# Ordering a two-layer hybrid decoder step on the compiler's detailed timing model instead of its simple one

## Chip, cores and metric

The kernel runs on one NeuronCore of a Trainium2 chip, as one program in one launch. The metric is the device time of an execution in microseconds (us); lower is better. The five engines have a stream of instructions each, and work through it in the order in which the compiler put it: TensorE (PE, with PEld for its weight loads), VectorE (DVE), ScalarE (ACT), GpSimd (POOL) and SyncE (SP, which issues most of the DMAs).

## What is computed

One inference step of two decoder layers for a prompt of 1024 tokens and 8 samples of one token each (1032 columns in all), width 1024, everything in float32.

```python
# layer 0
h = rmsnorm(x) @ w_in0                 # 4 HGRN2 heads of 128, 8 forgetting-attention (FoX) heads of 64
o = concat(hgrn2(h), fox(h)) @ w_out0  # hgrn2: chunked recurrence; samples: one step on a cached 128x128 state
x = x + o                              # fox: causal attention with a decay; samples: 512 cached positions each
x = x + convffn(rmsnorm(x))            # 2816 channels, gated, causal depthwise convolution of width 3
# layer 1
u = glu(rmsnorm(x) @ w_pw1)
u = swish(layernorm(dwconv31(u)))      # causal depthwise convolution of width 31
x = x + u @ w_pw2
x = x + convffn(rmsnorm(x))
y = rmsnorm(x)
```

The outputs are y for prompt and samples, and the new caches and states.

## The kernel before

**Matrix products.** Activations lie with channels on partitions and tokens along the row. Each float32 operand is split into a rounded high part and the rest: `split` (L104 to L106) makes the high part `wh` with an ACT copy (L105) and the low part `wl` with a subtraction on DVE or POOL (L106). A product is then three matmuls, high by high, high by low and low by high. Weights come in tiles `wr` of 1024x128 (SP DMA, L110, two buffers); the output weights of the ConvFFNs are `wor`, split into `oh` and `ol`. In the input projection of layer 0 the matmuls are those of L143, tiles `mm` of 512 or 260 columns with three PSUM buffers; from then on they are those of `dense2` (L1034 for the first 512 columns, L1037 for the other 520 in two pieces of 260) and of the ConvFFN's second product (L1175, L1184).

**Work under the dense tiles.** All else is "side work", written as Python generators. Between dense tiles the program takes steps from them at a rate set by hand:

```python
def step(self, n=1.0):                       # L191, class Side
    self.due = min(self.due + n, 2 * n)
    while self.due > 0 and self.q:
        self.due -= self.one()
```

In layer 0's mixer (0 to about 660 us) side work is the attention of four pairs of heads (scores L478 to L483, softmax on DVE L484, transposes L504, weighting L518 to L521), then the recurrence of four HGRN2 heads. Each of these heads has a dense part, whose three results `hf`, `hv` and `hq` are copied out by ACT (L589) into tiles that exist once (pool `hgd`, one buffer), so that the next head's copies wait for the last reader of this head's. The recurrence takes a decay chain on DVE (L645 to L694, with `kl` written at L685), transposes of `kl` (L704), products `pa` (L709, L711), a mask on POOL (L716), outputs `hpo` (L735, L737), and at its end the step for the samples, twice four samples: `vb` (DVE, L748), the product `sp3` (PE, L752), the new states `st` (DVE, L758, four instructions) and the products with `hq` (PE, L763, four columns of `sp2`), after which ACT copies `sp2` out (L766). The samples' attention runs beside it: gathers on POOL (L563), a product and a reduction on DVE over the cached keys (L781, L783), and the values (L883).

Later stages are the gates and the output projection (to about 760 us), the ConvFFN of layer 0 (`mlp`, L1116 to L1227) for either half of the tokens, the GLU and the convolution (taps on POOL L1277/L1278 and on DVE L1287/L1289), and the ConvFFN of layer 1. Means over the channels are matmuls: `mean` (L1042 to L1048) sends each piece of 260 columns through one PSUM buffer, and ACT copies it back to `ha` (L1048) before the next piece may be written:

```python
ps = one("dacc", "mean")                     # L1046
PE.matmul(ps[:, :z - o], mean_d, acc[:, o:z], start=True, stop=True)
ACT.copy(acc[:, o:z], ps[:, :z - o])         # L1048
```

**What sets the order.** The Python code says in which order instructions are issued, and the tile framework doesn't keep to it. When the `TileContext` is left (L1460), it puts the instructions of each engine in order, on a model of how long each takes and when its inputs and buffers are free, and then sets the semaphores. So the order on an engine follows from that model, and the hand-written rates are only its input.

## Time and profile before

| | us |
|---|---|
| median of 3 runs (lowest, highest) | 2617.6 (2612.87, 2620.34) |
| profiled execution, from first to last instruction | 2622.4 |
| PE busy in it | 2518.7 (96%) |
| PEld busy | 2223.7 (85%) |
| DVE busy | 1798.5 (69%) |
| ACT busy | 1232.2 (47%) |
| POOL busy | 746.8 (28%) |

The span of the profiled execution is the only time of its own that is known; it lies 4.8 us above the median. An engine is busy while one of its instructions runs; the rest of its span it waits for another engine, for a DMA or for its turn. Where PE is busy at half the clock, its work takes twice as long, so that busy time and useful time differ. The column PEclk of the profile shows that.

### The profile page before, as it was taken

The numbers are of one execution on the slowest core, as the hardware profiler recorded it, in microseconds if no ns is written. First come the engines' busy times: TensorE is split into PE (matmuls) and PEld (weight loads), VectorE is DVE, ScalarE is ACT, GpSimd is POOL, SyncE is SP. The second block draws the span as 40 slices with busy tenths as digits, with TensorE's granted clock in tenths as the row PEclk, the third lists the DMA queues.
The fourth block names the chain that finished last, engine by engine and source line by source line (L and its number), as shares of the span: only waits on it lengthen the run. The fifth ranks groups of instructions, "written<-read, shape, count | busy, mean of one in ns | idle before, by whom it ended". The sixth has DMA issues, their size and how long they took to land.

```text
span 2622.4 us, 40803 instructions
## 1 busy us (share of the span) xinstructions
PE 2518.7 (96%) x15857; PEld 2223.7 (85%) x15857; DVE 1798.5 (69%) x3138; ACT 1232.2 (47%) x2119; POOL 746.8 (28%) x714
## 2 busy tenths in 40 slices
PE   7999998998999999999999999999999999999998
PEld 7788887876787888797799999997777798999997
DVE  7676668776565555577999566759999656655455
ACT  5455565654454333345454345545554643333332
POOL 2011225325131111115664131046664101111111
PEclk9999999999999999999999999999999999999999
DMA  6212225334433333323232322333233323333321
GB/s 200 68 57 57 66 74 151 96 94 144 139 105 98 97 96 96 96 66 104 81 92 87 92 83 72 95 93 101 77 89 97 96 82 102 113 93 90 89 83 59
DMA packets 319908, 247.07 MB, mean 94 GB/s; under 512 B 12055, under 2 KB 292039, under 8 KB 319683
## 3 DMA queue, kind: packets, MB, share of 16 engines
q1 hardware_dynamic: 308899, 213.09, 27.7%
q0 software_dynamic: 10816, 31.38, 4.0%
q8 instruction: 125, 2.05, 0.3%
q14 instruction: 68, 0.56, 0.1%
HBM read 226.82 MB, written 18.73 MB: 94 GB/s over the span
## 4 chain that ended last, share of the span: by engine, by line
PE 70%; DVE 13%; DMA 6%; issue 5%; POOL 3%; ACT 3%; SPq 0%; POOLq 0%; DVEq 0%; ACTq 0%
PE mm L1037 21%; PE mm L1034 15%; PE mm L143 10%; PE mm L1184 9%; PE mm L1175 7%; DVE wl L106 3%; DVE dacc L1289 2%; DMA wr<-in_w_ffn_in 2%; PE sc L480 1%; DMA wor<-in_w_ffn_out 1%; PE tp L504 1%; DVE ga L1147 1%; POOL x L563 1%; DMA x<-in_cache_fox_v,idx 1%; POOL ol L106 1%
## 5 line engine op out<-in xcount | busy, mean ns | idle before, releaser
L105 ACT CAST wh<-wr 128x512 fp32r<-128x512 f32 x536 | 326.5, 617 | 689.9 <-PE mm L1037 266.9
L1037 PE MATMUL mm<-xn,wh 128*128 128x260 f32 x3840 | 624.2, 284 | 3.2 <-DVE U L1371 2.0
L106 DVE TENSOR_TENSOR wl<-wr,wh 128x512 fp32r<-128x512 f32 x512 | 407.9, 801 | 292.7 <-ACT wh L105 287.2
L1034 PE MATMUL mm<-xn,wh 128*128 128x512 f32 x1792 | 559.4, 393 | 2.9 <-ACT wh L105 2.4
L1037 PEld LDWEIGHTS mm<-xn,wh 128*128 128x128 f32 x3840 | 527.2, 188 | 7.8 <-issue 3.1
L106 POOL TENSOR_TENSOR ol<-wor,oh 128x512 fp32r<-128x512 f32 x176 | 245.2, 1413 | 752.6 <-ACT oh L105 440.7
L1034 PEld LDWEIGHTS mm<-xn,wh 128*128 128x128 f32 x1792 | 338.0, 189 | 75.1 <-ACT wh L105 3.3
L1037 PE MATMUL mm<-xn,wl 128*128 128x260 f32 x1920 | 387.0, 283 | 0.0
L143 PE MATMUL mm<-xn,wh 128*128 128x260 f32 (+2 forms) x1584 | 384.9, 330 | 0.5 <-ACT qraw L311 0.5
L1034 PE MATMUL mm<-xn,wl 128*128 128x512 f32 x896 | 352.9, 394 | 13.1 <-DVE wl L106 13.0
L1037 PEld LDWEIGHTS mm<-xn,wl 128*128 128x128 f32 x1920 | 295.9, 188 | 0.2 <-DVE wl L106 0.2
L143 PEld LDWEIGHTS mm<-xn,wh 128*128 128x128 f32 x1584 | 268.2, 192 | 26.9 <-issue 7.5
L143 PE MATMUL mm<-xn,wl 128*128 128x260 f32 (+2 forms) x792 | 260.8, 329 | 0.0
L1278 POOL TENSOR_TENSOR dp<-dp,s 128x512 f32<-128x512 f32 x144 | 202.0, 1403 | 115.3 <-ACT s L1277 105.4
L1289 DVE SCALAR_TENSOR_TENSOR dacc<-U,wdw,dacc 128x512 f32<-128x512 f32 x304 | 227.8, 749 | 4.4
L1034 PEld LDWEIGHTS mm<-xn,wl 128*128 128x128 f32 x896 | 169.3, 189 | 55.0 <-DVE wl L106 19.8
L1147 DVE SCALAR_TENSOR_TENSOR ga<-gx,wfd,ga 128x544 f32<-128x544 f32 (+1 forms) x176 | 143.4, 815 | 46.7 <-ACT ga L1145 44.4
L1092 DVE TENSOR_TENSOR x<-x,mm 128x520 f32<-128x520 f32 x176 | 121.0, 692 | 67.8 <-PE mm L1184 60.9
L143 PEld LDWEIGHTS mm<-xn,wl 128*128 128x128 f32 x792 | 151.9, 192 | 13.8 <-issue 4.1
L105 ACT CAST oh<-wor 128x512 fp32r<-128x512 f32 x176 | 104.6, 618 | 115.9 <-DMA wor<-in_w_ffn_out 51.1
L1175 PE MATMUL mm<-ah,oh 128*128 128x512 f32 x352 | 139.8, 399 | 12.0 <-DVE ga L1157 7.3
L1184 PE MATMUL mm<-ah,oh 128*128 128x260 f32 x672 | 137.7, 286 | 8.1 <-DVE ga L1159 4.0
(378 smaller groups left out, 4018.0 us busy)
## 6 DMA issues: line engine op xcount, KB each, us to landing
wr<-in_w_ffn_in SPq DMA_DIRECT2D x176, 512.0 KB
wor<-in_w_ffn_out SPq DMA_DIRECT2D x88, 512.0 KB
wr<-in_w_pw SPq DMA_DIRECT2D x48, 512.0 KB
wr<-in_w_in SPq DMA_DIRECT2D x28, 512.0 KB
wr<-in_w_out SPq DMA_DIRECT2D x16, 512.0 KB
xt<-in_x_prompt SPq DMA_DIRECT2D x8, 512.0 KB
xtd<-xs POOLq DMA_DIRECT2D x8, 512.0 KB, 5.3
cb<-cumd SPq DMA_DIRECT2D x8, 512.0 KB
```

The costliest lines, as they stand in the source:

```text
L105: ACT.copy(h, raw)
L106: (eng or DVE).tensor_tensor(out=l, in0=raw, in1=h.bitcast(F32), op=ALU.subtract)
L143: PE.matmul(ps, a[k], b[:, k, :], start=k == order[0] and j == 0, stop=k == order[-1] and j == 2)
L480: PE.matmul(sc[:, :nn], ql[r, sl], tk[r, h, k0:k0 + nn], start=False, stop=k0 + n < W)
L1034: PE.matmul(ps[:, i], a[k], xt[:, r, k], **f)
L1037: PE.matmul(ps[:, q, 0:260], a[k], xt[:, r, k, q * 260:q * 260 + 260], **f)
L1092: DVE.tensor_tensor(out=ways(x[:, m, sl], h), in0=ways(x[:, m, sl], h), in1=outs(ps, h), op=ALU.add)
L1147: DVE.scalar_tensor_tensor(out=ga, in0=gx[:, t:t + m], scalar=wd[t], in1=ga, op0=ALU.mult, op1=ALU.add)
L1175: PE.matmul(ps[:, q], o[m + q], a, start=i == 0, stop=i == len(js) - 1)
L1184: PE.matmul(ps[:, q, 0:260], o[m], a[:, q * 260:q * 260 + 260], start=i == 0, stop=i == len(js) - 1)
L1278: POOL.tensor_tensor(out=dps[k], in0=dps[k], in1=q, op=ALU.add)
L1289: ins = DVE.scalar_tensor_tensor(out=o, in0=src, scalar=w, in1=accs[k], op0=ALU.mult, op1=ALU.add)
```

## The change

The context is opened with another timing model. Comments and docstrings are blanked as well, which leaves the line numbers as they were; the first of those is shown.

```diff
     def cs(c):
-        """one piece of the tokens"""
+
         return slice(PC[c][0], sum(PC[c]))
...
-    with tile.TileContext(nc) as tc:
+    with tile.TileContext(nc, schedule_with_timeline_sim=True) as tc:
         tile_hybrid_step(tc, *args)
```

The computing instructions are the same in both programs, one for one: 15671 on PE, 3138 on DVE, 1973 on ACT, 717 on POOL and 491 on SP. What follows from the order differs: ACT loads its function tables 69 times instead of 63, and DVE has 710 instructions that only wait for a semaphore instead of 624. The order differs on every engine and in all parts of the program. Three places follow.

PE at the end of the first HGRN2 head's recurrence (about 421 to 430 us before). `mm_...` are dense tiles, `sp3` and `sp2` the samples' step, `st` and `vb` its inputs from DVE, `hms` a mean for the head's norm. Before:

```order
L752 MATMUL sp3_4909<-vb_4907,kv8_4674 128x512
L618 MATMUL hms_5012<-hsq_4980,mean_h_79 128x260
L143 MATMUL mm_5041<-xn1_100,wl_4927 128x260
L763 MATMUL sp2_4906<-hq_4486,st_4911 128x1
L143 MATMUL mm_5041<-xn1_100,wh_4925 128x260 x2
L143 MATMUL mm_5041<-xn1_100,wl_4927 128x260
L763 MATMUL sp2_4906<-hq_4486,st_4911 128x1
```

With the change:

```order
L143 MATMUL mm_5143<-xn1_100,wl_5077 128x260
L656 MATMUL sp1_5242<-ident_70,hk_5215 8x128
L657 MATMUL sp1_5242<-ident_70,hv_4922 8x128
L737 MATMUL hpo_4895<-qe_4817,S_4891 128x128
L752 MATMUL sp3_4909<-vb_4907,kv8_4674 128x512
L618 MATMUL hms_5012<-hsq_4980,mean_h_79 128x260
L763 MATMUL sp2_4906<-hq_4486,st_4911 128x1 x4
L752 MATMUL sp3_4966<-vb_4964,kv8_4674 128x512
L763 MATMUL sp2_4906<-hq_4486,st_4968 128x1 x4
L143 MATMUL mm_5189<-xn0_99,wh_5181 128x512 x2
L143 MATMUL mm_5189<-xn0_99,wl_5183 128x512
```

The dense matmuls that stood between the parts of the samples' step now stand ahead of it or behind it, so that sp3, sp2, sp3 and sp2 follow each other with nothing between them but one mean.

PE at the transposes of `kl` in the second head (455.8 us before; `mm_5317`, `mm_5400` and `mm_5530` are dense tiles, `kl` comes from DVE). Before:

```order
L143 MATMUL mm_5317<-xn1_100,wl_5184 128x260
L143 MATMUL mm_5400<-xn1_100,wh_5181 128x260 x2
L143 MATMUL mm_5400<-xn1_100,wl_5183 128x260
L143 MATMUL mm_5400<-xn1_100,wh_5181 128x260
L704 MATMUL htp_5269<-ident_70,kl_5247 128x128 x4
```

With the change:

```order
L711 MATMUL pa_5384<-qd_5360,kX_5372 128x64
L143 MATMUL mm_5530<-xn1_100,wl_5472 128x260
L143 MATMUL mm_5530<-xn1_100,wh_5470 128x260 x2
L704 MATMUL htp_5269<-ident_70,kl_5247 128x128 x4
L143 MATMUL mm_5530<-xn1_100,wl_5472 128x260
```

The transposes now stand behind the rest of mm_5400, all of a tile mm_5477 and three quarters of mm_5530, about two and a half dense tiles later; the tile's products pa stand ahead of them.

ACT in the first norm of layer 1's ConvFFN (about 2040 to 2050 us before; `mean_20220` is the first piece of a mean over the channels, `wr_20372` a weight tile from a DMA). Before:

```order
L105 CAST ah_20153<-ga_20105 128x512
L105 CAST wh_20374<-wr_20372 128x512
L105 CAST wh_20375<-wr_20372 128x512
L1130 COPY gx_20211<-mm2_20186 128x512
L1048 COPY ha_20023<-mean_20220 128x260
L1145 ACTIVATE ga_20215<-gx_20211,bfd_93,wfd_92 128x512
```

With the change:

```order
L105 CAST ah_20153<-ga_20105 128x512
L1130 COPY gx_20211<-mm2_20186 128x512
L1048 COPY ha_20023<-mean_20220 128x260
L105 CAST wh_20374<-wr_20372 128x512
L105 CAST wh_20375<-wr_20372 128x512
L1145 ACTIVATE ga_20215<-gx_20211,bfd_93,wfd_92 128x512
```

The copies of gx and of the mean now stand ahead of the two casts of the weight tile instead of behind them. On PE the second piece of the mean, which needs the first one's copy, now stands 15 rows behind the first piece instead of 4, with dense matmuls between.

## Rows read from the trace of the kernel before

**Rows 1.** Windows of core 0: busy us of each engine (instructions), PEclk, DMA share, GB/s; the sum.

```profile
391.00:460.00 69.00, 60.96 (x373) 52.63 (x374) 56.67 (x86) 38.97 (x68) 36.27 (x31) 0.93 0.53 152
460.00:664.00 204.00, 185.44 (x1087) 149.66 (x1088) 148.33 (x252) 109.51 (x176) 80.58 (x69) 0.96 0.39 114
...
800.00:1100.00 300.00, 300.00 (x1316) 246.65 (x1315) 154.35 (x203) 110.34 (x185) 54.07 (x55) 1.00 0.34 100
...
1792.00:2000.00 208.00, 195.64 (x842) 156.57 (x841) 205.35 (x261) 103.61 (x177) 121.02 (x97) 1.00 0.30 88
...
sum 2622.40, PE 2518.67 PEld 2223.70 DVE 1798.55 ACT 1232.17 POOL 746.81; mean PE 125.93 PEld 111.18 DVE 89.93 ACT 61.61 POOL 37.34
```

**Rows 2.** Timeline of PE, 96 to 112 us: start, us, instruction, [idle before <-releaser].

```profile
98.81 1.14 PE L438 MATMUL tps<-ident,kraw 128*128 128x128 f32 x8 [1.08 <-ACT vt L439]
100.86 0.27 PE L449 MATMUL tps<-ident,qraw 128*8 128x128 f32 x1 [0.91 <-ACT kt L439]
...
101.84 1.22 PE L143 MATMUL mm<-xn,wh 128*128 128x512 f32 x2 [0.49 <-ACT qraw L311]
```

**Rows 3.** Timeline of PE in the HGRN2 heads, 455 to 600 us.

```profile
455.83 1.11 PE L704 MATMUL htp<-ident,kl 128*128 128x128 f32 x4 [5.71 <-DVE kl L685]
...
574.96 0.66 PE L704 MATMUL htp<-ident,kl 128*128 128x128 f32 x4 [3.19 <-DVE kl L685]
599.56 0.49 PE L735 MATMUL hpo<-at,hvt 128*128 128x128 f32 x2 [3.15 <-POOL at L716]
```

**Rows 4.** Timeline of PE at the first head's samples, 421 to 430 us.

```profile
421.10 1.12 PE L752 MATMUL sp<-vb,kv 8*128 8x512 f32 x2
...
429.20 0.28 PE L763 MATMUL sp<-hq,st 128*128 128x1 f32 x2
```

**Rows 5.** Timeline of DVE, 424 to 441 us.

```profile
425.13 0.43 DVE L148 SCALAR_TENSOR_TENSOR hya<-hms,hy 128x260 f32<-128x260 f32 x1 [1.17 <-ACT hy L102]
425.48 1.21 DVE L783 TENSOR_REDUCE sal<-x 128x16 f32<-128x1024 f32 x1
426.61 1.11 DVE L758 SCALAR_TENSOR_TENSOR st<-st,frs,sp 128x128 f32<-128x128 f32 x4
427.63 0.42 DVE L149 TENSOR_TENSOR hya<-hya,hy 128x260 f32<-128x260 f32 x1
429.42 1.23 DVE L781 TENSOR_TENSOR x<-x 128x1024 f32<-128x1024 f32 x1 [1.37 <-issue]
```

**Rows 6.** Timeline of ACT and of PE at the mean, 2040 to 2056 us.

```profile
2046.65 1.14 ACT L105 CAST wh<-wr 128x512 fp32r<-128x512 f32 x2 [4.19 <-DMA wr<-in_w_ffn_in]
...
2048.60 1.24 PE L1047 MATMUL mean<-ha,mean_d 128*128 128x260 f32 x2 [5.88 <-ACT ha L1048]
```

**Rows 7.** Timeline of PE, 1776 to 1792 us.

```profile
1784.23 0.96 PE L1034 MATMUL mm<-xn,wh 128*128 128x512 f32 x2 [2.05 <-ACT wh L105]
1786.55 0.80 PE L1034 MATMUL mm<-xn,wl 128*128 128x512 f32 x1 [1.36 <-DVE wl L106]
```

**Rows 8.** Windows at half the clock, columns as in rows 1.

```profile
101.80:112.04 10.24, 10.20 (x25) 6.04 (x26) 4.62 (x21) 3.53 (x11) 1.20 (x3) 0.50 0.50 168
453.40:460.20 6.80, 4.37 (x19) 3.83 (x19) 5.52 (x12) 4.84 (x12) 0.23 (x1) 0.50 0.21 71
2047.40:2054.20 6.80, 5.59 (x13) 4.45 (x14) 5.08 (x9) 6.03 (x10) 0.10 (x1) 0.50 0.27 81
1784.60:1791.40 6.80, 5.44 (x13) 3.80 (x12) 6.80 (x10) 3.70 (x7) 3.20 (x3) 0.50 0.26 84
```

**Rows 9.** Timeline of PE, two smaller waits.

```profile
762.68 0.71 PE L1047 MATMUL mean<-ha,mean_d 128*128 128x260 f32 x2 [1.77 <-ACT ha L1048]
...
2167.57 0.50 PE L1034 MATMUL mm<-xn,wl 128*128 128x512 f32 x1 [2.16 <-DVE wl L106]
```

**Rows 10.** ACT's table loads by line; DVE's waits at L758 (ns min/median/max).

```profile
L102 ACT ACT_TABLE_LOAD x48 | 61.6, 1283 | 0.8
...
L758 DVEq EVENT_SEMAPHORE  x8: 21/21/50, 419.4 to 612.8; - x8
```

## The prediction

> **What bounds the kernel now.** The table of windows comes first: PE is busy 2518.67 of 2622.40 us, so that 103.7 us of idle time is all that a better order of unchanged work could take out of PE's gaps [rows 1]. The same table says where it cannot come from: between 800 and 1100 us PE is busy for all 300.00 us. There a new order can only lose. The idle time lies in a few places: 8.0 us between 391 and 460 us and 18.6 us between 460 and 664 us (the HGRN2 heads), and 12.4 us between 1792 and 2000 us, where DVE is busy 205.35 of 208 us and sets the pace. The second view is the timeline of PE with the releasers of its waits: it shows what each gap waited for [rows 2 to 4, 6, 7, 9]. The third is the granted clock by windows. Behind several of these gaps PE runs at 0.50, the lower level of 1.2 GHz, for 6.8 to 10.2 us [rows 8]. Work that is done in such a stretch takes twice its time, so a stretch costs half of its busy time on top of the gap: 5.1, 2.2, 2.8 and 2.7 us for the four shown.
>
> So the question for each moved instruction is what stands ahead of it on PE, and whether that is enough to cover the engine it waits for.
>
> **What the new order takes away.**
>
> 1. *The step from the projections to the first attention.* PE waits three times, for 1.08, 0.91 and 0.49 us, in sum 2.5 us, and then works 10.2 us at half clock [rows 2, 8]. With the change score matmuls of the attention and part of a dense tile stand between these transposes. Bounds: 0 and 2.5 + 5.1 = 7.6 us. I take 5, since the engines that PE waits for keep their queues and may be late by a part of it.
>
> 2. *The transposes of kl.* PE waits 5.71 us for DVE and runs the next 4.37 us of work at half clock, 2.2 us more [rows 3, 8]. They now stand about two and a half dense tiles later, which is longer than the wait. Bounds 0 and 7.9 us; I take 6, near the whole, and leave the rest for the product pa, which now stands ahead of the transposes and waits for the same DVE chain. The second such wait is 3.19 us, and the one for POOL's mask 3.15 us [rows 3]: 6.3 us together, upper bound with a clock stretch like the 2.2 above for each 10.7 us. The order moves them less clearly, so I take 4, with 0 as lower bound.
>
> 3. *The mean in layer 1's ConvFFN.* ACT waits 4.19 us for a weight tile's DMA, casts it for 1.14 us, and only then copies the mean for which PE idles 5.88 us [rows 6]. With the copy ahead of the casts nothing keeps it, and the second piece of the mean also has 14 rows of dense work ahead of it. The casts themselves are not urgent: their first reader on PE stands some 60 rows further on. 5.88 + 2.8 us for the clock [rows 8] is 8.7 us; I take 8, bounds 0 and 8.7.
>
> 4. *The weights at 1784 us.* Two waits of 2.05 and 1.36 us for ACT's casts and DVE's subtraction, and 5.44 us at half clock, which costs 2.7 [rows 7, 8]: 6.1 us as upper bound. The casts and subtractions move ahead of convolution taps on ACT and DVE. I take 4, because the casts also waited for their DMA, which an order on ACT alone doesn't hasten; lower bound 0.
>
> 5. *Small ones.* The mean of the first ConvFFN waits 1.77 us, a low part of weights 2.16 us [rows 9]; both stand further behind what they need. Upper bound 3.9; I take 3.
>
> In sum 5 + 6 + 4 + 8 + 4 + 3 = 30 us, with an upper bound of 7.6 + 7.9 + 10.7 + 8.7 + 6.1 + 3.9 = 44.9.
>
> **What it adds.**
>
> 6. *The samples' step at a head's end.* Before, the chain from the first sp3 (421.10 us) to the last product with hq (429.20 + 0.28) takes 8.4 us, and dense matmuls cover it [rows 4]. Now they stand ahead of it or behind it, so PE can only wait. I work out the wait from DVE's rows: the new states take 1.11 us; then, ahead of the second four, DVE has vb, a product of 1.23, 0.43, 1.21 and 0.42 us, and the states again at 1.11 [rows 5]. Without vb (which lies beside PE's own sp3) that is 1.11 + 3.29 + 1.11 = 5.5 us, less the 1.12 us of the second sp3 [rows 4], which PE does meanwhile: 4.4 us. The same holds at the ends of the first three heads, behind which another head's dense work is held up by hq, for which there is one buffer: 3 x 4.4 = 13 us. Bounds: nothing, if DVE lags less behind PE than assumed, and 3 x (8.4 + 2.2 for a clock stretch) = 31.8 us.
>
> 7. *Attention.* Dense tiles run ahead of side work there too, and at three places scores, transposes and weightings follow each other with no dense matmul between for 8 to 11 us of PE's work. No row shows such a place without cover. The nearest are the 1.08 us wait at its start [rows 2] and the 5.71 us wait of the recurrence [rows 3], for bounds of 0 and 3 x 5.7 = 17 us. I take 1 us for each, 3 in all, because attention has several independent blocks in flight and resembles the first row more.
>
> 8. *Layer 0's ConvFFN, second half.* The second product stands closer behind the x that it needs, by about 1 us of PE's work at some places; 2 us, with 0 and twice the 2.16 us of a wait for a DVE result [rows 9], 4.3 us, as bounds.
>
> 9. *At no cost:* six more table loads at 1283 ns [rows 10] are 7.7 us on ACT, which is idle half of the span; they would count at up to 7.7 where ACT is late. 86 more waiting instructions on DVE at 21 to 50 ns [rows 10] are 1.8 to 4.3 us, hidden outside 1792 to 2000 us, where perhaps a fifth of them fall: under 1 us. Weight loads, gathers and the moves of DMAs on SP's queue are covered by the two buffers of the weight tiles as before; if that cover is gone, the wait is like the 4.19 us of [rows 6], once. The last gaps in the DVE-bound stage stay.
>
> In sum 13 + 3 + 2 = 18 us. The net is 30 - 18 = 12 us less. Against the profiled execution's 2622.4 us that is 2610.4; this execution lies 4.8 us above the median of the runs, so I forecast 2617.6 - 12 = **2605.6 us**.
>
> **Rivals.** A difference of 0.3%, 7.9 us, is about what a measurement of this kernel can tell from none.
>
> *The clock takes the gain back.* A gap of 5.71 us was followed by 6.8 us at half clock, and so was the shorter one of 2.05 us [rows 3, 7, 8]. If each of the three head ends and the three places in attention is followed by such a stretch, at 2.2 us each, 13 us are lost and the time is about 2605.6 + 13 = 2619 us: no difference. The Trainium skill speaks for this: TensorE: Matmul & The Clock Gate, Part 1, says that the array falls to half rate when it has been idle and must work for a while to be back at full rate; it follows that six short gaps may cost more than two long ones. The trace agrees as far as it goes, with 0.50 behind the gaps named. Against it: the many small gaps between 1792 and 2000 us, 12.4 us in all, go with a granted clock of 1.00 [rows 1]. Chance 0.22, with the case that the gaps of steps 1 and 2 only move to the next wait of their chain.
>
> *Slower: uncovered side work.* One buffer for hq, hf and hv and three for dense tiles set how far dense work can run ahead; what it did early is missing as cover later. If the head ends cost 31.8 us and attention 10, in place of 16, the net is 12 - 25.8, 14 us slower: 2631 us. For it speaks that the HGRN2 stage already loses 26.6 us with work interleaved finely [rows 1]; against it, that moving dense tiles between kl and its transposes helps the same heads. With attention at 10 us it decides from head ends of (13 + 12 + 7.9 - 7) / 3 = 8.6 us each, near the whole 8.4 us of the chain and so without any cover. Chance 0.23.
>
> *Nothing reaches the path.* The order changes but waits stay, since DVE and DMAs set the times of those gaps: within a few us of 2617.6. It would need the mean at 2048 us to wait still, which I think unlikely; it is in the 0.22 above.
>
> **How the numbers follow.** Forecast 0.55, no difference 0.22, slower 0.23. The lower end is all gains and half of the losses, 2617.6 - 44.9 + 9 = 2582, say 2580; the upper end takes in the slower rival with a few us more, 2635. Faster by over 0.3% means below 2609.7; the forecast lies close to it, so that a part of its chance falls to no difference, and an equal part comes back from gains nearer their upper bounds.
>
> **What would show it.** Right: the mean at about 2048 us without a wait of over 1 us and no half clock there; PE's idle time at L704 below 2 us; new waits of 4 to 5 us of L763 for DVE's st, L758, three times; PE's idle time between 391 and 664 us about as now, 26.6 us, since these waits replace those at L704. Wrong: a wait of PE for ACT or a DMA in the stretch from 800 to 1100 us, which is now full; idle time in attention over 10 us; or head ends of over 8.6 us each, with which the kernel is slower.

## The result and the profile after

The changed kernel takes 2683.3 us (median of 4 runs, 2673.5 to 2700.8) where the kernel before takes 2619.0 us on the same chip: a ratio of 1.0246, interval 1.0217 to 1.0276. It is 2.5% slower, 64 us, and lies above the range of the prediction. Built and run again as `after_again` it took 2673.2 us, ratio 1.0225 (1.0194 to 1.0256), so two measurements put the loss between 1.9 and 2.8%.

The page of the changed kernel, span, busy times and the granted clock by slices:

```profile
span 2671.8 us, 40905 instructions
...
PE 2539.1 (95%) x15857; PEld 2246.5 (84%) x15857; DVE 1797.1 (67%) x3138; ACT 1235.5 (46%) x2125; POOL 762.3 (29%) x714
...
PEclk9999998889999999999999999999999999999999
```

The span grew by 2671.8 - 2622.4 = 49.4 us against the profiled execution of before [rows 1]; the rest of the 64 us is that the latter lies above its median and this one below. The 49.4 us have two parts. PE's idle time went from 103.7 to 132.7 us, 29.0 more. And PE is busy 20.4 us longer with the same matmuls (15857 in either profile): by the mean granted clock, 0.972 and 0.988 before, it stands at half clock for some 149 us, 63 us before, and three slices in a row show an 8. DVE and ACT are busy as long as before, POOL 15.5 us longer.

What PE waited for, by line and releaser (us in all, times, longest), first lines and some further down:

```profile
PE mm L1184 <- DVE x L1092: 19.7, 10, 4.2
PE mm L1175 <- DVE ga L1157: 18.9, 6, 5.8
PE mm L1175 <- DVE x L1176: 9.8, 3, 5.1
PE ps L268 <- DVE y L157: 9.8, 1, 9.8
...
PE sp L752 <- DVE S L729: 4.5, 1, 4.5
PE mm L1034 <- DVE wl L106: 4.2, 3, 2.1
...
PE htp L704 <- DVE hya L148: 3.7, 1, 3.7
...
PE sp L763 <- DVE st L758: 3.3, 4, 1.4
...
PE mean L1047 <- ACT ha L1048: 1.4, 1, 1.4
```

And the same view of the kernel before:

```profile
PE mm L1034 <- DVE wl L106: 13.0, 13, 2.2
PE htp L704 <- DVE kl L685: 9.5, 3, 5.7
...
PE mean L1047 <- ACT ha L1048: 7.7, 2, 5.9
PE mm L1175 <- DVE ga L1157: 7.3, 6, 2.8
...
PE mm L1175 <- DVE x L1176: 4.7, 4, 2.0
...
PE mm L1184 <- DVE x L1092: 2.6, 1, 2.6
```

The reader sees an exchange. The waits that the prediction wanted gone are gone or small: for the low parts of weights (L1034), for kl (L704), for the mean (L1047). In their place PE waits in the second product of the ConvFFNs (L1175 for the first 512 columns, L1184 for the rest) for DVE: for the gate (L1157) and for the additions into x (L1092, L1176), 48.4 us in place of 14.6. The prediction named one of these places, L1184 in layer 0, in its step 8, with a price of 2 us. The 18.9 us for the gate all lie between 1800 and 2060 us of the changed kernel, where it forecast a loss of under 1 us.

### The profile page after: what moved, and what is told of

Read it like the earlier page. It is cut to its first block, busy times and chain, and to the rows that moved or that the text cites. A ratio compares the mean times of both kernels' runs of the same rounds, so it can differ in the third digit from the quotient of the medians.

```text
span 2671.8 us, 40905 instructions
## 1 busy us (share of the span) xinstructions
PE 2539.1 (95%) x15857; PEld 2246.5 (84%) x15857; DVE 1797.1 (67%) x3138; ACT 1235.5 (46%) x2125; POOL 762.3 (29%) x714
## 4 chain that ended last, share of the span: by engine, by line
PE 74%; DVE 10%; DMA 5%; issue 5%; ACT 3%; POOL 2%; SPq 0%; POOLq 0%; DVEq 0%; ACTq 0%
PE mm L1037 23%; PE mm L1034 16%; PE mm L143 11%; PE mm L1184 8%; PE mm L1175 7%; DVE wl L106 2%; DMA wr<-in_w_ffn_in 2%; DVE dacc L1289 2%; DMA wor<-in_w_ffn_out 2%; PE sc L480 1%; DVE ga L1147 1%; PE tp L504 1%; ACT wh L105 1%; PE sc L478 1%; PE po L519 1%
## 5 line engine op out<-in xcount | busy, mean ns | idle before, releaser
L106 DVE TENSOR_TENSOR wl<-wr,wh 128x512 fp32r<-128x512 f32 x512 | 401.7, 790 | 340.2 <-ACT wh L105 336.9
L1034 PE MATMUL mm<-xn,wh 128*128 128x512 f32 x1792 | 555.0, 391 | 0.2 <-DVE x L1176 0.2
L1034 PEld LDWEIGHTS mm<-xn,wh 128*128 128x128 f32 x1792 | 336.8, 188 | 70.9 <-issue 0.6
L1034 PE MATMUL mm<-xn,wl 128*128 128x512 f32 x896 | 350.6, 391 | 4.2 <-DVE wl L106 4.2
L1278 POOL TENSOR_TENSOR dp<-dp,s 128x512 f32<-128x512 f32 x144 | 200.6, 1393 | 126.5 <-ACT s L1277 120.6
L1289 DVE SCALAR_TENSOR_TENSOR dacc<-U,wdw,dacc 128x512 f32<-128x512 f32 x304 | 227.7, 749 | 3.2
L1034 PEld LDWEIGHTS mm<-xn,wl 128*128 128x128 f32 x896 | 168.5, 188 | 41.8 <-DVE wl L106 6.3
L1147 DVE SCALAR_TENSOR_TENSOR ga<-gx,wfd,ga 128x544 f32<-128x544 f32 (+1 forms) x176 | 148.6, 844 | 44.8 <-ACT ga L1145 43.9
L1175 PE MATMUL mm<-ah,oh 128*128 128x512 f32 x352 | 144.5, 412 | 28.7 <-DVE ga L1157 18.9
L1092 DVE TENSOR_TENSOR x<-x,mm 128x520 f32<-128x520 f32 x176 | 121.4, 692 | 70.5 <-PE mm L1184 61.2
L1184 PE MATMUL mm<-ah,oh 128*128 128x260 f32 x672 | 143.2, 295 | 21.6 <-DVE x L1092 19.7
```

Source lines behind the costliest of these rows:

```text
L106: (eng or DVE).tensor_tensor(out=l, in0=raw, in1=h.bitcast(F32), op=ALU.subtract)
L1034: PE.matmul(ps[:, i], a[k], xt[:, r, k], **f)
L1092: DVE.tensor_tensor(out=ways(x[:, m, sl], h), in0=ways(x[:, m, sl], h), in1=outs(ps, h), op=ALU.add)
L1147: DVE.scalar_tensor_tensor(out=ga, in0=gx[:, t:t + m], scalar=wd[t], in1=ga, op0=ALU.mult, op1=ALU.add)
L1175: PE.matmul(ps[:, q], o[m + q], a, start=i == 0, stop=i == len(js) - 1)
L1184: PE.matmul(ps[:, q, 0:260], o[m], a[:, q * 260:q * 260 + 260], start=i == 0, stop=i == len(js) - 1)
```

## Experiments

**How the order was set.** All kernels with an order of their own open the context as the changed kernel does and then chain the instructions of each engine in an order that a table gives. With the whole old order in it, this gives the order of the kernel before on every engine.

```diff
-    with tile.TileContext(nc) as tc:
+    with tile.TileContext(nc, schedule_with_timeline_sim=True) as tc:
         tile_hybrid_step(tc, *args)
+        in_order(tc, nc, TABLE)
...
+    for deltas in json.loads(zlib.decompress(base64.b85decode(table))):
+        n, last = 0, None
+        for d in deltas:
+            n += d
+            i = by[f"I-{n}"]
+            if last is not None:
+                tc.add_manual_dep(i, last.name, info, reason="in_order")
+            last = i
```

So most edits below are a choice of what stands in the table. Each ratio is to the kernel before on the same chip.

**Which part loses.** `after_again` is the changed kernel, unedited. `mixer_before` has the old order for layer 0's mixer (up to the output projection at about 660 us) and the new one behind it; `rest_before` the other way round. `attention_new` has the new order only for what is issued ahead of the first HGRN2 head.

> The changed kernel once more, for a second trace. Its runs differ by 27 us. If the granted clock makes that difference, a trace with a span other by d has TensorE busy at half clock for about 2 d longer or shorter, with the waits themselves alike; if waits make it, the idle time differs by d.

> Layer 0's mixer (the first 664 us) in the old order on all engines, everything behind it in the new order. If the loss sits in the mixer (samples' steps and attention without dense matmuls around them), most of the 64 us come back and the time is within 20 us of the kernel before, about 2635. If it sits in the ConvFFNs and the convolution, where VectorE reads finished PSUM tiles later, only the mixer's share of the profiled difference (19 of 49 us) comes back: 2650 to 2665, with TensorE's waits for VectorE at the second products of the ConvFFNs (L1184 and L1175) as in the changed kernel, 40 to 50 us.

> The reverse: the mixer in the new order, everything behind it in the old order. If the mixer holds the loss: 2660 to 2680. If the ConvFFNs hold it: 2635 to 2645, with TensorE's waits at L1184 and L1175 below 25 us as before the change. If the two parts add up, this kernel's excess over the kernel before and that of the run with the old mixer sum to the changed kernel's.

> Only the instructions traced ahead of the first HGRN2 head's dense tiles (norms, the attention's projections and most of the attention) in the new order, the recurrence and all that follows in the old one. The whole mixer in the new order cost 27 us. If the ends of the heads (stretches of 15.6, 22.6 and 13.1 us without a dense matmul) make most of it, this run is within 10 us of the kernel before: 2619 to 2629. If the attention's stretches of 17.8, 10.0 and 20.5 us make it: 2635 to 2645.

| | median us | ratio to before |
|---|---|---|
| after_again | 2673.2 | 1.0225 (1.0194 to 1.0256) |
| mixer_before: new behind the mixer | 2657.4 | 1.0155 (1.0125 to 1.0186) |
| rest_before: new in the mixer | 2645.4 | 1.0100 (1.0071 to 1.0129) |
| attention_new: new in the first part of the mixer | 2632.1 | 1.0054 (1.0036 to 1.0073) |

In us over the medians of before: 38.7 behind the mixer and 26.7 in it, 65.4 together. The whole lost 64.3 at first and 54.5 in after_again, on the chip of these two runs. Each loss is known to within about 8 us, so that the two parts add up to the whole as far as can be told. The second trace of the changed kernel is 3.5 us shorter than the first, all of it idle time of PE; what makes its runs differ by 27 us such a small difference doesn't tell. Of the 26.7, 12.8 lie ahead of the first head, and so about 14 in the heads. A part of the 12.8 is at the very start, which the prediction passed over. In attention_new, PE's waits up to 420 us:

```profile
PE ps L268 <- DVE y L157: 9.4, 1, 9.4
PE tp L504 <- DVE tl L106: 4.8, 2, 4.0
```

From PE's first instruction to the one that stood at 54 us before, attention_new takes 52.6 us and the kernel before 48.8.

**Which stage behind the mixer.** `second_new` has the old order everywhere but in the second half of layer 0's ConvFFN (some 1180 to 1590 us), the stage of the prediction's step 8.

> The old order everywhere but in the second half of layer 0's ConvFFN (about 1180 to 1590 us), which has the new order on every engine. If this stage alone holds the loss behind the mixer, the kernel is 20 to 38 us slower, 2638 to 2656 us, with PE waiting for DVE's additions at L1092 and gates at L1157 as in the changed kernel. Rival, the loss comes in from the stages ahead (work that the new order left undone there): under 10 us, below 2628.

Measured: 2653.0 us against 2624.0, ratio 1.0117 (1.0097 to 1.0136), 25 to 36 us slower, where the whole part behind the mixer lost 38.7. So this stage alone can make most of that loss, but between two stages in the old order it loses more than in its own surroundings: from PE's instruction at 1180 us before to the one at 1590 it is 37.8 us longer in second_new's profiled execution, 25.6 in that of mixer_before and 14.1 in that of the changed kernel. On PE the edit is small: one tile of the second product stands ahead of most of a dense tile, and the rest is mostly small transposes (L1141) that stand elsewhere. On DVE it is larger; one piece:

```diff
-L1136 COPY gx<-ghist 128x2
 L1143 COPY gx<-hps 128x8x2
 L1139 COPY glast<-mm_11262 128x10
 L1142 COPY gx<-mm_11262 128x8
-L106 TENSOR_TENSOR wl<-wr,wh 128x512
-L1147 SCALAR_TENSOR_TENSOR ga<-gx,wfd,ga 128x544
-L106 TENSOR_TENSOR wl<-wr,wh 128x512
-L1147 SCALAR_TENSOR_TENSOR ga<-gx,wfd,ga 128x544
+L1147 SCALAR_TENSOR_TENSOR ga<-gx,wfd,ga 128x544 x2
```

What PE then waits for can be followed in the timeline of second_new, DVE from 1328.6 us, POOL beside it, and PE's one wait:

```profile
1328.64 0.68 DVE L106 TENSOR_TENSOR wl<-wr,wh 128x512 fp32r<-128x512 f32 x1
...
1329.24 0.74 DVE L1289 SCALAR_TENSOR_TENSOR dacc<-U,wdw,dacc 128x512 f32<-128x512 f32 x1
...
1329.76 3.00 POOL L1278 TENSOR_TENSOR dp<-dp,s 128x512 f32<-128x512 f32 x2 [2.40 <-ACT s L1277]
1329.90 1.74 DVE L1147 SCALAR_TENSOR_TENSOR ga<-gx,wfd,ga 128x544 f32<-128x544 f32 x1
...
1331.56 0.74 DVE L1289 SCALAR_TENSOR_TENSOR dacc<-U,wdw,dacc 128x512 f32<-128x512 f32 x1
1332.22 1.12 DVE L1147 SCALAR_TENSOR_TENSOR ga<-gx,wfd,ga 128x544 f32<-128x544 f32 x1
1333.27 0.68 DVE L106 TENSOR_TENSOR wl<-wr,wh 128x512 fp32r<-128x512 f32 x1
...
1333.87 0.74 DVE L1289 SCALAR_TENSOR_TENSOR dacc<-U,wdw,dacc 128x512 f32<-128x512 f32 x1
1334.53 0.68 DVE L1092 TENSOR_TENSOR x<-x,mm 128x520 f32<-128x520 f32 x1
...
1335.27 0.80 PE L1184 MATMUL mm<-ah,oh 128*128 128x260 f32 x2 [3.83 <-DVE x L1092]
```

PE has worked off the tiles for which it had PSUM buffers at about 1331 us. DVE comes to the addition at 1334.53, since from 1329.90 on two taps of the convolution (L1289), two of the gate (L1147) and a weight split stand ahead of it in its queue, 4.6 us in all, and PE's next tile has no buffer until it is done. The two of the gate take 1.74 and 1.12 us beside POOL's additions (L1278), where the median of L1147 is 0.78, so that 1.3 of the 4.6 us go with POOL. DVE doesn't pause here: the windows of second_new and, for the stage as it was, of the kernel before (columns as in [rows 1]) show it full.

```profile
1325.00:1337.00 12.00, 8.17 (x62) 7.94 (x61) 12.00 (x19) 4.63 (x8) 4.39 (x3) 0.92 0.28 88
```

```profile
1330.00:1440.00 110.00, 106.69 (x872) 105.18 (x872) 106.00 (x176) 52.92 (x87) 59.28 (x43) 1.00 0.30 88
```

Already before, DVE was busy 106 of the 110 us, and PE 106.69. Neither has room there. The windows of the whole stretch, second_new from the instruction at 1330 us before to those at 1440 and 1590, and the kernel before from 1440 us on:

```profile
1330.39:1454.67 124.28, 112.95 (x873) 111.55 (x872) 114.84 (x178) 51.73 (x86) 61.64 (x44) 0.93 0.26 79
1454.67:1620.53 165.86, 154.21 (x1215) 151.36 (x1214) 93.28 (x163) 69.42 (x109) 35.63 (x28) 0.96 0.27 77
```

```profile
1440.00:1590.00 150.00, 149.27 (x1216) 146.83 (x1215) 90.60 (x163) 65.35 (x104) 35.59 (x28) 1.00 0.29 86
```

Of the 30 us that these two windows are longer, 19 are idle time of PE, and 11 are busy time that is longer with the same instructions, at a clock of 0.93 and 0.96 in place of 1.00. Half of the loss lies behind 1440 us, where DVE has room again. The longest wait of all is there, behind a block of eight subtractions (L1328); first second_new, then the same block in the changed kernel:

```profile
1460.30 9.22 DVE L1328 TENSOR_TENSOR U<-U,hy 128x512 f32<-128x512 f32 x8
1470.18 0.80 PE L1184 MATMUL mm<-ah,oh 128*128 128x260 f32 x2 [6.49 <-DVE x L1092]
```

```profile
1475.92 4.90 DVE L1328 TENSOR_TENSOR U<-U,hy 128x512 f32<-128x512 f32 x8
```

In second_new POOL is at work beside most of the block, in the changed kernel beside its end only, and the longest idle time of PE behind it there is 0.65 us. What comes late on DVE is therefore both what stands ahead of it in the queue and how long that takes beside POOL. How much of the loss is the latter was not tried.

**Is it the place of a few instructions in DVE's queue?** `prompt_reads` is the changed kernel with 129 of DVE's readers of PSUM (L1092, L1157, L1176 and others) up to 9 rows earlier. `gating_first` moves the whole gating chain ahead, in the same way, as far as its inputs had been ready in the changed kernel's trace. One place of DVE's order in prompt_reads, and one in gating_first:

```diff
-L106 TENSOR_TENSOR xn_7597<-s,xn_7597 128x512 x2
+L106 TENSOR_TENSOR xn_7597<-s,xn_7597 128x512
+L1092 TENSOR_TENSOR x<-x,mm_7547 128x520
+L106 TENSOR_TENSOR xn_7597<-s,xn_7597 128x512
 L1084 SCALAR_TENSOR_TENSOR s<-x,pv,hy 128x512 x2
-L1092 TENSOR_TENSOR x<-x,mm_7547 128x520
```

```diff
-L1147 SCALAR_TENSOR_TENSOR ga<-gx,wfd,ga 128x512
 L1084 SCALAR_TENSOR_TENSOR s<-x,pv,hy 128x520
+L1147 SCALAR_TENSOR_TENSOR ga<-gx,wfd,ga 128x512 x2
+L1084 SCALAR_TENSOR_TENSOR s<-x,pv,hy 128x520 x3
```

> The changed kernel with one thing moved: behind the mixer, 129 VectorE instructions that read a finished PSUM tile (the residual additions L1092 and L1176, the gating products L1157 and L1159) stand up to nine rows earlier on VectorE, where by the changed kernel's trace their inputs were done; no other engine's order is touched. If late reads of PSUM are what stops TensorE there, its waits at L1184 and L1175 fall from 51 us to under 25 and the time by 20 to 40 us against the changed kernel, to 2645 to 2660. If VectorE is simply full or the second products wait for something else, the waits only change their names and the time stays within 8 us of the changed kernel.

> The new order on every engine but DVE; on DVE, behind the mixer, the whole chain of a ConvFFN tile (the taps of width 3 at L1147, the products at L1157 and L1159, the additions at L1092 and L1176, and the small copies for the samples) stands ahead of splits and convolution taps that were not needed earlier by anyone, as far up as its own inputs were ready in the changed kernel's trace. If the place of these steps in DVE's queue is the cause of the loss in the second half, 15 to 30 us faster than the changed kernel, 2645 to 2665 us. Rival, it takes ACT's order too, since the Gelu between L1147 and L1157 stays where it is: within 8 us of the changed kernel, 2670 to 2688.

prompt_reads: 2679.9 us, ratio 1.0228 (1.0207 to 1.0250). gating_first: 2693.3 us, ratio 1.0248 (1.0223 to 1.0273). Both are misses: neither gains on the changed kernel. The waits of gating_first, first those of PE, then of DVE:

```profile
PE mm L1184 <- DVE x L1092: 31.0, 13, 5.6
PE mm L1175 <- DVE ga L1157: 17.4, 6, 5.6
...
DVE glast L1139 <- ACT gx L1137: 128.1, 40, 5.8
```

Moved ahead, the chain makes DVE itself wait for ACT's copy of gx, 40 times, and what stands behind it waits too. In the changed kernel that wait is 5.8 us, once. So moving DVE's steps alone, in these two ways, does not bring the loss back. That what comes early on DVE must be early on ACT as well is what this suggests; the runs of the next part test it.

**Is it one engine's order?** Mixer old in all of them. Behind it one or more engines have the old order, the others the new one.

> The mixer in the old order on all engines; behind it only VectorE's order is the old one, and the detailed model puts the other engines in order. With every engine new behind the mixer the time was 2657, with every engine old 2619. If VectorE's order (taps of the convolution and weight remainders ahead of the chain that gates a ConvFFN tile) makes the loss, most of the 38 us come back: below 2632. If TensorE's, ScalarE's or the queues' order makes it, 2645 to 2660.

> The same with only TensorE's order the old one behind the mixer. If the transposes of the samples' history (L1141), which now stand in the second products, or any other place of TensorE's matmuls make the loss: below 2632. If VectorE's order makes it: 2645 to 2660, with the waits at L1184 and L1175 still there.

> The same with only ScalarE's order the old one behind the mixer. If ScalarE (its casts of weights, the activations of a tile and the products for POOL's taps) is the engine whose place decides: below 2632. If VectorE's order alone makes the loss: 2645 to 2660.

> The mixer in the old order; behind it VectorE's and ScalarE's orders are the old ones, TensorE, POOL and SyncE are put in order by the detailed model. A tile's gating goes from ScalarE to VectorE and back (L1145, L1147, the Gelu, L1157), so if the loss is that these two no longer fit each other, both together bring it back though neither did alone: below 2630. If TensorE's order or the queue of the weight DMAs has to fit as well: 2640 to 2665.

> The same with TensorE's order old as well; only POOL's and SyncE's orders (the low parts ol, the convolution's taps on POOL, the DMAs of the weights) are left to the detailed model. If the three compute engines hold the whole loss: within 6 us of the kernel before, about 2619. If the order of the DMA queue or of POOL counts too: above 2630, with ScalarE's waits for weight DMAs longer than the 161 and 51 us before.

The last four columns are us of the profiled execution between the same instructions of PE, those that started at 1330, 1440, 1590, 1778 and 2000 us before:

| old behind the mixer | median us | ratio to before | 1330 to 1440 | to 1590 | to 1778 | to 2000 |
|---|---|---|---|---|---|---|
| everything (before) | | 1 | 110.0 | 149.9 | 188.0 | 221.9 |
| nothing (mixer_before) | 2657.4 | 1.0155 (1.0125 to 1.0186) | 123.0 | 168.0 | 185.8 | 227.3 |
| DVE | 2671.5 | 1.0189 (1.0130 to 1.0247) | 119.6 | 153.3 | 214.4 | 229.1 |
| PE | 2658.7 | 1.0144 (1.0102 to 1.0185) | 120.8 | 163.9 | 191.4 | 223.1 |
| ACT | 2661.4 | 1.0160 (1.0118 to 1.0201) | 114.2 | 161.8 | 207.7 | 232.4 |
| DVE, ACT | 2638.5 | 1.0069 (1.0050 to 1.0088) | 111.5 | 149.7 | 208.1 | 221.5 |
| PE, DVE, ACT | 2622.7 | 0.9997 (0.9983 to 1.0011) | 110.0 | 149.0 | 188.2 | 225.0 |

No engine's old order alone brings anything back. With DVE's and ACT's together the stage from 1330 to 1590 us is as it was (261.2 us, 259.9 before), with PE's order still the new one there. What is then still lost are new waits between 1590 and 1778 us, where the mixture of two orders gives PE 14 us of idle time that neither whole order has. With PE's order too all is back. POOL's and SP's new orders behind the mixer cost nothing that can be measured.

**The prediction's single steps, each alone on the old order.** `kl_late` moves only the transposes of kl at 455.8 us behind 20 dense matmuls (step 2). `samples_close` moves the dense matmuls away from the samples' step at the ends of the first three heads (step 6). `mean_ahead` moves the mean's copy ahead of the casts at 762 and 2048 us, and the second piece of the mean five dense matmuls on (step 3). `three_moves` is kl_late, the same at 575 us behind 12 matmuls, and the mean at 2048 us. One piece of each edit: PE in kl_late, PE in samples_close, ACT in mean_ahead and three_moves.

```diff
-L143 MATMUL mm<-xn_100,wh 128x260
+L143 MATMUL mm<-xn_100,wh 128x260 x2
+L143 MATMUL mm<-xn_100,wl 128x260
...
 L704 MATMUL htp<-ident,kl 128x128 x4
-L143 MATMUL mm<-xn_100,wh 128x260
```

```diff
 L752 MATMUL sp_4909<-vb,kv_4674 128x512
 L618 MATMUL hms<-hsq,mean_h 128x260
...
-L763 MATMUL sp_4906<-hq,st 128x1
...
+L763 MATMUL sp_4906<-hq,st 128x1 x4
 L752 MATMUL sp_4966<-vb,kv_4674 128x512
```

```diff
+L1048 COPY ha<-mean 128x260
 L105 CAST wh<-wr 128x512 x2
 L1130 COPY gx<-mm_20186 128x512
-L1048 COPY ha<-mean 128x260
 L1145 ACTIVATE ga<-gx,bfd,wfd 128x512
```

> The old order on every engine but PE, and there only the transposes of kl at 455.8 us behind the remaining 20 matmuls of the dense tile that they stood in, some 6 us of work. The prediction's step 2: the wait of 5.71 us goes, and the half clock behind it, 6 us faster, about 2612 us. Rival, the head's chain sets the pace: the wait goes from this place and comes back behind it, within 3 us of the kernel before.

> The old order on every engine but PE, and there only the samples' step at the ends of the first three HGRN2 heads as the change has it: sp3, four products, sp3, four products with no dense matmul between; the 19, 12 and 28 dense matmuls of the tiles begun there stand ahead of the first sp3, the rest behind the last product. The prediction's step 6: three waits of about 4.4 us, 13 us slower, about 2631 us. Rival, a head's own chain through DVE sets the pace of this stage: PE's waits appear but dense work was only waiting anyway, within 4 us of the kernel before, 2614 to 2622.

> The kernel before in its own order with one thing taken from the change: the copy of the first piece of the mean (L1048) stands ahead of the casts that wait for a weight DMA, at 762 and at 2048 us, and the second piece's matmul five matmuls later. If the gain forecast for the mean was right and was only outweighed by losses elsewhere: 6 to 11 us faster than the kernel before, 2608 to 2613, and no wait of TensorE at L1047 over 1 us. If the wait only moves to the weights that the casts prepare: within 3 us of the kernel before.

> The old order but for three moves: the transposes of kl at 455.8 us behind 20 dense matmuls (as in kl_late), those at 575 us behind 12, and the mean at 2048 us as the change has it. kl_late measured 0.15% faster. By the prediction's prices 6 + 2 + 8 us faster, about 2602 us; by what kl_late and mean_ahead gave, 4 to 8 us faster, 2610 to 2614; rival, nothing that can be told from the kernel before.

| | median us (before) | ratio to before |
|---|---|---|
| kl_late | 2619.7 (2624.0) | 0.9985 (0.9973 to 0.9997) |
| samples_close | 2630.3 (2624.0) | 1.0032 (1.0019 to 1.0045) |
| mean_ahead | 2617.3 (2621.5) | 0.9993 (0.9980 to 1.0006) |
| three_moves | 2617.7 (2624.3) | 0.9973 (0.9959 to 0.9987) |

kl_late gains some 4 us, though the wait doesn't go; it shrinks from 5.71 us [rows 3]:

```profile
454.15 1.11 PE L704 MATMUL htp<-ident,kl 128*128 128x128 f32 x4 [3.42 <-DVE kl L685]
```

samples_close loses some 8 us. Its new waits are shorter than foreseen, from its trace:

```profile
PE sp L763 <- DVE st L758: 5.6, 4, 1.8
```

The rest of its loss goes with the clock: between the instructions that stood at 406 and 664 us before, it runs 51 us at half clock where the kernel before ran 24. Which of the two leads was not taken apart. mean_ahead takes the wait for the mean away and the stage from 2000 to 2060 us is 8.7 us shorter (51.4 in place of 60.1), as forecast. The next stage, up to 2200 us, is 7.4 us longer (147.3 in place of 139.9): PE now comes sooner to weights whose low parts are not ready, and the wait for them grows by 2.9 us from the 13.0 shown above:

```profile
PE mm L1034 <- DVE wl L106: 15.9, 13, 3.0
```

The half clock moves with it: from 2060 to 2100 us the granted clock is 0.93, where from 2058 to 2100 us it was 1.00.

three_moves is the fastest of all kernels here against its own runs of before: 0.27% (0.13 to 0.41), some 7 us.

**Does the half clock cost time?** `fill_waits` has the old order, and in five of PE's waits in the heads matmuls whose results nobody reads, so that PE doesn't stand still.

```diff
+KL, PO, SX = {2: 22, 6: 12}, {7: 12}, {6: 16, 7: 12}
...
+    for _ in range(counts.get(k, 0)):
+        FILL.append(PE.matmul(out, w, x, start=True, stop=True).ins.name)
```

> The kernel before in its own order, with matmuls added whose result nobody reads, at five of TensorE's waits in the recurrence and the samples' attention: 22 and 12 of 512 columns ahead of the transposes of kl at 456 and 575 us, 12 ahead of the outputs at 600 us, 16 and 12 small ones ahead of the products at 645 and 658 us. They take about as long as TensorE waits there. If the half clock behind a wait costs time by itself, the stretches at half clock at these five places (24 us) go, the mean granted clock rises by 0.002 to 0.004 and the time falls by 4 to 10 us, though TensorE has more to do. If the waits alone cost time, the time stays within 3 us of the kernel before or rises.

Measured: 2616.1 us against 2617.7, ratio 0.9997 (0.9983 to 1.0012). The stretch of the heads in its windows, which showed 185.44 busy and 0.96 [rows 1]:

```profile
460.00:664.00 204.00, 196.98 (x1196) 161.28 (x1196) 155.36 (x259) 114.20 (x183) 83.75 (x71) 1.00 0.41 124
```

The clock is full there, and the kernel as a whole gains nothing that can be measured. That does not show that half clock is free, since the first group of added matmuls waits itself, is at half clock until 454.5 us and takes longer than the wait of 5.71 us that it fills:

```profile
448.67 8.04 PE L40 MATMUL pa<-xn 128*128 128x512 f32 x22 [2.89 <-DVE kv L691]
```

From PE's instruction at 406 us before to the transposes of kl at 455.8 this trace takes 53.7 us, from there to the instruction at 664 us 199.3. In the traces of the nine kernels that have the mixer in its old order, unedited, the two stretches take 48.4 to 51.9 and 203.2 to 210.4 us. In the second one these nine stand at half clock for 14 to 33 us, the fastest of them least and the slowest most. So the half clock does seem to cost some us in the heads, and the added matmuls seem to take back what they gain; in one execution each, that is not settled.

## Why the prediction was wrong

The steps below carry the prediction's numbers.

**The step that failed is 8, layer 0's ConvFFN, second half:** "2 us, with 0 and twice the 2.16 us of a wait for a DVE result [rows 9], 4.3 us, as bounds". Alone it costs 25 to 36 us (second_new). The prediction counted how much of PE's work lay between a product and "the x that it needs", and took DVE to be on time. In the changed kernel's own trace the stage is 14.1 us longer. The product does not need that x either; it waits for the buffer that the addition into x reads. The prediction named the stretch from 1792 to 2000 us as the one that DVE sets, and made nothing of the windows of this stage, in which DVE was busy for 106 of 110 us already before. With DVE full there, an instruction that is put ahead of L1092 can make it later by its whole length, 4.6 us in the piece shown, and the half clock behind such waits adds to them. The bound for step 8 should have been such a piece for many tiles, not two waits.

**Step 9, "at no cost", left out what mattered.** For POOL's and SP's queues behind the mixer it held; the six table loads were not tried alone. But it costed only instructions that were added and DMAs that were moved. From 1330 to 1590 us the loss goes with the orders of DVE and ACT together, and exchanging one of them alone gains nothing over the whole, as the table of engines shows.

**Step 6, the samples' step:** 13 us forecast, 0.32% or some 8 us measured alone, inside the bounds. The waits are 1.4 us each and not 4.4; the stretches at half clock grew by 27 us. **Step 7, attention:** 3 us forecast, with 17 as bound; 12.8 measured for all that lies ahead of the heads, a part of it at the start of the program.

**Step 2, kl:** the gain is there, smaller. 6 us forecast, 4 measured alone (1 to 7), with 2.3 us of the wait of 5.71 covered. In the changed kernel no wait for kl is left, but the heads lose some 14 us; the forecast for them was 13 lost at step 6 and 10 gained at step 2. **Step 3, the mean:** the wait nearly went (1.4 us in all is left of 7.7), but alone (mean_ahead), by the ratio, only 1.8 us (-1.6 to 5.2) of the 8 reach the end. The term failed because the next stage was taken as given: PE there waits for the weights' low parts, and the wait and the half clock move to that place. **Steps 1, 4 and 5** were not tried alone. Of the waits at 98 to 102 us [rows 2] 0.6 us are left in the changed kernel's trace, and those at 1784 us [rows 7] are gone. What stands some 25 us behind the place of the latter, from PE's timeline of the changed kernel:

```profile
1844.24 0.79 PE L1175 MATMUL mm<-ah,oh 128*128 128x512 f32 x1 [5.81 <-DVE ga L1157]
```

The stage from 1778 to 2000 us takes 228.6 us in the changed kernel, 221.9 before. There too DVE's gate is late, in the stage that the prediction itself called bound by DVE.

**The rivals.** "Slower: uncovered side work" had the sign, and PE's idle time, but its place and its price were wrong: it made three buffers and the heads decide. The heads cost less than its 8.6 us each, and the larger part of the loss lies behind the mixer, where it named nothing. "The clock takes the gain back" is half true. The half clock did grow, from 63 to some 149 us. The Trainium skill's rule, that the array falls to half rate when it has been idle, made one expect that (TensorE: Matmul & The Clock Gate, Part 1), and the trace agrees where it shows waits: at the one of 5.81 us above the clock is 0.50 from 1843 to 1850 us. The clock is a part of the loss: the busy time of PE grew by 20.4 us in the changed kernel, and by 11 us in second_new's stage. What half clock costs in the heads fill_waits leaves open. Of the tests that the prediction set itself, the idle time of PE between 391 and 664 us came out as said, 26.8 us, but with other waits in it. The waits of L763 came to 3.3 us in four, not three of 4 to 5; L704 kept one of 3.7 us, not for kl; the mean kept one of 1.4 us, with no half clock. "Idle time in attention over 10 us" did not come (4.6 us between 60 and 385 us), nor a wait for ACT or a DMA between 800 and 1100 us. One for DVE did, with the same name as the others:

```profile
814.10 0.79 PE L1175 MATMUL mm<-ah,oh 128*128 128x512 f32 x1 [5.08 <-DVE x L1176]
```

**What stays open.** Which instructions of DVE and of ACT must change place together to save the stage from 1330 to 1590 us was not found: two ways of moving DVE's alone failed. How much of the loss comes from DVE's instructions that take longer beside POOL was not tried, and how much of the heads' 14 us is wait and how much is clock was not taken apart either.

## What to carry to other kernels

When an order changes as a whole, ask for each stage which engine has no room, by its windows, before looking at PE's gaps; where a second engine is as full as PE, an instruction that is put ahead of a reader of PSUM can become a wait of PE of its whole length. Moving such readers alone did not bring the time back here; the orders of two engines had to go back together. A wait that is taken away counts only if the stage behind it can use the time: of 8.7 us at the mean 7.4 were lost again a stage later. And a change that loses as a whole can be taken apart: three small moves out of thousands, put on the old order, gave 0.27%.

## What the chip showed that was not expected

**A small copy of DVE that waits out an instruction of POOL.** L1136 copies two columns and takes 0.17 us in the median of the changed kernel; four of its 44 take 1.27 us and one 0.97, and in the kernel before one takes 1.05. From the changed kernel's timeline:

```profile
1340.50 0.92 DVE L106 TENSOR_TENSOR wl<-wr,wh 128x512 fp32r<-128x512 f32 x1
1340.84 3.01 POOL L106 TENSOR_TENSOR ol<-wor,oh 128x512 fp32r<-128x512 f32 x2
1341.34 1.27 DVE L1136 COPY gx<-ghist 128x2 f32<-128x2 f32 x1
1342.53 0.16 DVE L1143 COPY gx<-hps 128x16 f32<-128x16 f32 x1
1342.61 0.74 DVE L1289 SCALAR_TENSOR_TENSOR dacc<-U,wdw,dacc 128x512 f32<-128x512 f32 x1
```

POOL's first instruction of the two ends at 1342.59 us and the copy at 1342.61; the other four long ones end within 0.03 us of an instruction of POOL as well. In neither kernel does a copy of L1136 end ahead of an instruction of POOL that had begun before it. The tap behind it (L1289), whose accumulator lies in PSUM, runs beside POOL's second instruction at its usual 0.74 us. The Trainium skill says that DVE and GpSimd share one pair of SBUF ports, and that for a DVE instruction in a two-port mode, which a copy can enter, the one that issues later is blocked for the whole of the other's instruction (SBUF — State Buffer, Who interferes with whom). The copy agrees with that; the tap does not show it. The five copies take 5.2 us more of DVE than five short ones, between 1341 and 1460 us of the changed kernel. That they reach PE is not shown.

**Half clock on a busy PE.** From 515 to 535 us of the changed kernel, in windows (columns as in [rows 1]):

```profile
515.00:520.00 5.00, 5.00 (x28) 4.43 (x26) 3.66 (x8) 0.59 (x1) 0.98 (x1) 0.55 0.58 157
520.00:525.00 5.00, 4.91 (x15) 2.76 (x15) 2.97 (x11) 2.29 (x3) 0.59 (x1) 0.50 0.04 13
525.00:530.00 5.00, 5.00 (x16) 3.26 (x14) 3.27 (x9) 2.18 (x3) 0.77 (x1) 0.50 0.18 52
530.00:535.00 5.00, 3.81 (x13) 3.27 (x13) 4.03 (x15) 3.27 (x8) 1.42 (x2) 0.50 0.37 105
```

PE is busy 18.72 of 20 us and the clock stays at 0.50, its level of 1.2 GHz. It had fallen at 515 us, behind the wait of 3.7 us at L704 shown above, and is back at 539 us, 6 us into the dense matmuls that follow. From 510.5 to 533.1 us no dense matmul stands: the instructions are transposes, the recurrence's and the samples' products, and products of one column. The prediction looked for half clock behind gaps; here it begins behind one and stays where PE shows hardly any.
